# A third stage of seven block products for four recurrent heads, weight sums added up in DRAM, and outputs that may wait for their gates

## The chip, the cores and the metric

The kernel runs on one core of a Trainium2 chip. The metric is the device time of one execution in microseconds (us). A core has five engines with queues of their own: TensorE (PE, matmuls; PEld is its loading of the stationary operand), VectorE (DVE), ScalarE (ACT), GpSimd (POOL) and SyncE (SP). Here SP issues loads and POOL issues stores; both go to the same 16 DMA engines. Matmuls write to PSUM, which this kernel uses as eight tiles of 128x512 words (banks); everything else lies in SBUF or in DRAM.

## The reference

One layer over 1024 tokens of width 1024 in float32. A normalised and modulated input `h` goes through one wide projection. Two recurrences run on its pieces, HGRN2 (8 heads of 128) and GLA (4 heads, keys of 128, values of 256). Each result is normalised, gated and projected, and the two are merged.

```python
h = rms_norm(x, norm_w[l]) * (1.0 + scale[:, None, :]) + shift[:, None, :]
proj = h @ w_in[l]
hq, hf, hi, hz, gq, gk, gv, gz, ga, mg = jnp.split(proj, IN_OFFSETS, axis=-1)
y_h = hgrn2_branch(hq, hf, hi, hz, lb_all[l], hgrn_norm_w[l])
y_g = gla_branch(gq, gk, gv, gz, ga, gla_alpha_w[l], gla_alpha_b[l], gla_norm_w[l])
u_h = y_h @ w_branch[l, 0]
u_g = y_g @ w_branch[l, 1]
mg = jax.nn.sigmoid(mg.reshape(B, T, N_BRANCH, D_MODEL))
merged = mg[:, :, 0] * u_h + mg[:, :, 1] * u_g
x = x + gate[:, None, :] * (merged @ w_out[l])
return rms_norm(x, final_norm_w)
```

In HGRN2 the query is `silu(hq)`, the forget gate `f = lb + (1 - lb) * sigmoid(hf)`, the key `(1 - lb) * sigmoid(-hf)`, and the normalised output is multiplied by `silu(hz)`. GLA's output is multiplied by `silu(gz)`.

## The kernel before

Every large product is taken three times on operands split into a high and a low part (`hi`, `lo`): hi x hi, hi x lo, lo x hi. Making a split costs a cast on ScalarE (`pinned_split`, line 211) and a subtraction on VectorE (line 212). `h` stays split in SBUF, in 16 tiles of `N_SLOTS` = 46 of 4 KB per partition (`Slots`: the slot that was freed longest ago is given out first). A slot may be written again only when its last reader is done, a store included.

There are two ways to multiply. A *feature* (`Feat`, 128 columns of `w_in` for all tokens) takes 8 x 6 = 48 matmuls of 128x512 (line 607) and hands its two PSUM banks to `done`: a query or gate through `silu_done` (sigmoid on ScalarE, product on VectorE), a forget gate through `hf_done`. A *stage of seven block products* computes a 1024x1024 product by 2x2 blocks with seven multiplications instead of eight. For products 5, 3, 6, 7 it needs sums of weight blocks, for 5, 6, 7, 4 differences of blocks of `h`. A stage is 14 jobs (`Vjob`: product `p`, half `kk` of the depth) of 24 matmuls (line 1899). V0 (GLA's values) makes the differences on the way and stores them (`fx`); V1 (HGRN2's values) loads and splits them again. V1's weight sums are made by `v_sums` on VectorE and stored (`vs`).

The jobs run in the order of the list `J`. Beside it `stream.weave` steps two queues of generators, counted in units of six 128x512 matmuls. `stream.side` holds the attention of the 12 heads: scores of a head at four widths (lines 665, 698, 756 and 762, 767), transposes of the keys (791), states (813) and outputs (832, 834). An attention starts when its features are done; at its end `post` multiplies its output by the gate tile, and `put_act` stores it on POOL (`yg`, `yh`). `stream.back` holds work for later: `alpha_side`, `v_sums`, `prepare` and `gate_side`. `prepare` makes the weight sums of the four last stages: 16 times it loads two 512 KB blocks, adds on VectorE (lines 1195 to 1201) and issues four stores on POOL (`ws`, line 1203).

The last stages (`last_stages`, `GROUPS`, matmuls of line 1351) are four more stages of seven products: the two merge gates, then the two branch projections. Stage `b` = 0 fetches blocks of `h` and their differences (`fetch_factor`) and splits them (`build`). Its first two products still run beside the last head, whose score banks `sc_ps` the third, product 5, takes over (`scores_done`). `out_stage` does the output projection.

The scheduler orders the instructions of an engine by their place in the program and by what they need; `held` keeps one where the program has it. Each engine runs its list in order, so an instruction that waits holds all behind it. V0 runs from about 110 to 190 us, GLA's gates and keys to 310, V1 to 420, the last GLA gates and HGRN2 to 806, the last stages to 1110, the output to the end.

## Time and profile before

| what | before |
|---|---|
| median of three runs | 1177.17 us (1176.99 to 1177.36) |
| profiled execution | 1178.0 us |
| its span, first to last instruction | 1176.2 us |
| matmuls recorded | 8137 |
| DMA | 221.44 MB, mean 188 GB/s |
| HBM read, written | 154.57 MB, 65.54 MB |

The page gives for each engine its busy time, in 40 slices the tenths of busy time, and groups of instructions by line and tile: busy time, mean duration, and after the bar the idle time just ahead of them with what ended it. In a timeline a row has its start, its length and how many instructions it merges. A DMA's row gives the time on the issuing engine; its landing is a column of its own.

### The profile page before, as it was taken

The page shows a single profiled execution, that of the slowest core. Times are in us where ns is not written, and L with a number is a line of the kernel's source. Part 1 is how long each engine was busy: PE and PEld are TensorE (multiplying, and loading weights), DVE is VectorE, ACT ScalarE, POOL GpSimd, SP SyncE. Part 2 cuts the span into 40 slices and gives each one's busy share as a digit, 9 for nine tenths or more (in the row PEclk, how much of TensorE's full clock was granted, in tenths as well). Part 3 has the DMA queues.
Part 4 walks back from the last instruction along what each step waited for, and adds up shares of the span by engine and source line. Part 5 has one row for each costly group of instructions (what it writes and reads, how often), then busy time and mean ns, then how long its engine had stood idle before and what let it go on. Part 6 is the DMA issues. An engine that isn't in the chain of part 4 may idle for free.

```text
span 1176.2 us, 20432 instructions
## 1 busy us (share of the span) xinstructions
PE 1156.2 (98%) x8137; PEld 953.1 (81%) x8137; DVE 849.6 (72%) x1347; ACT 589.5 (50%) x903; POOL 125.0 (11%) x261
## 2 busy tenths in 40 slices
PE   7999999999999999999999999999999999999997
PEld 5777888888888788888888878888888888888886
DVE  4754778567665946897897798795643866988994
ACT  4675464663465535433433425567543644534654
POOL 4121111000100212111111010001110000000000
PEclk8999999999999999999999999999999999999999
DMA  9846445255675856565555453247699846434523
GB/s 319 279 149 233 161 170 189 77 165 171 207 260 177 279 189 201 171 203 173 174 184 188 134 205 112 91 162 241 196 314 298 274 156 215 130 108 162 187 90 134
DMA packets 150802, 221.44 MB, mean 188 GB/s; under 512 B 9052, under 2 KB 107410, under 8 KB 150707
## 3 DMA queue, kind: packets, MB, share of 16 engines
q1 hardware_dynamic: 132114, 158.37, 43.2%
q0 software_dynamic: 18544, 61.76, 13.6%
q8 instruction: 64, 1.05, 0.4%
q14 instruction: 32, 0.25, 0.1%
q10 hardware_dynamic: 48, 0.01, 0.0%
HBM read 154.57 MB, written 65.54 MB: 187 GB/s over the span
## 4 chain that ended last, share of the span: by engine, by line
PE 64%; issue 25%; DVE 4%; POOL 3%; DMA 2%; ACT 1%; SPq 0%; POOLq 0%; DVEq 0%; ACTq 0%
PE pd L607 16%; PE pd L1899 11%; PE pd L1351 9%; PE sc_ps L1351 5%; PE pm L1351 4%; PE pd L1528 3%; PE pd L396 3%; PE sc_ps L1528 2%; PE pm L832 1%; PE pm L1528 1%; POOL ws L1203 1%; PE sc_ps L396 1%; PE pm L834 1%; PE pm L813 1%; DMA b<-qk 1%
## 5 line engine op out<-in xcount | busy, mean ns | idle before, releaser
L607 PE MATMUL pd<-b,b 128*128 128x512 f32 x1632 | 391.1, 395 | 0.2 <-DVE b L212 0.2
L607 PEld LDWEIGHTS pd<-b,b 128*128 128x128 f32 x1632 | 302.1, 188 | 64.3 <-DVE b L212 0.6
L1351 PE MATMUL pd<-b,b 128*128 128x512 f32 x720 | 169.8, 390 | 0.1
L1899 PE MATMUL pd<-b,b 128*128 128x512 f32 x672 | 157.5, 393 | 2.6 <-ACT b L211 1.2
L1351 PEld LDWEIGHTS pd<-b,b 128*128 128x128 f32 x720 | 134.8, 188 | 28.5 <-ACT pd L1334 0.5
L1899 PEld LDWEIGHTS pd<-b,b 128*128 128x128 f32 x672 | 125.3, 188 | 30.5 <-ACT b L211 1.6
L212 DVE TENSOR_TENSOR b<-b,b 128x1024 fp32r<-128x1024 f32 x78 | 94.3, 1221 | 35.0 <-ACT b L211 34.7
L1294 DVE TENSOR_TENSOR b<-b,b 128x1024 fp32r<-128x1024 f32 x56 | 68.4, 1225 | 68.5 <-ACT b L1293 54.4
L1293 ACT CAST b<-b 128x1024 fp32r<-128x1024 f32 x56 | 58.5, 1049 | 69.5 <-PE pm L1351 17.0
L211 ACT CAST b<-b 128x1024 fp32r<-128x1024 f32 x78 | 79.8, 1047 | 12.1 <-DMA v<-b 3.9
L1351 PE MATMUL sc_ps<-b,b 128*128 128x512 f32 x324 | 77.2, 390 | 0.0
L1270 ACT CAST b<-b 128x1024 fp32r<-128x1024 f32 x48 | 49.7, 1049 | 46.5 <-PE pd L1351 16.0
L1351 PE MATMUL pm<-b,b 128*128 128x512 f32 x300 | 71.1, 389 | 0.0
L1351 PEld LDWEIGHTS sc_ps<-b,b 128*128 128x128 f32 x324 | 60.7, 188 | 12.6
L1271 DVE TENSOR_TENSOR b<-b,b 128x1024 fp32r<-128x1024 f32 x48 | 58.0, 1226 | 17.0 <-ACT b L1270 11.5
L1351 PEld LDWEIGHTS pm<-b,b 128*128 128x128 f32 x300 | 56.3, 188 | 11.7
L718 ACT COPY xb<-b 128x512 f32<-128x512 f32 x48 | 29.7, 621 | 55.8 <-DVE b L700 18.9
L1203 POOL DMA_DIRECT2D ws<-b x64 | 34.8, 545 | 190.6 <-DVE b L1195 118.7
L203 DVE TENSOR_TENSOR b<-b,b 128x1024 fp32r<-128x1024 f32 (+1 forms) x37 | 35.9, 984 | 26.4 <-ACT b L202 26.3
L396 PE MATMUL pd<-b,b 128*128 128x512 f32 x192 | 51.9, 403 | 0.5 <-ACT b L202 0.4
L832 PE MATMUL pm<-scT,b 128*128 128x128 f32 x256 | 46.9, 275 | 0.5 <-DVE b L819 0.5
L396 PEld LDWEIGHTS pd<-b,b 128*128 128x128 f32 x192 | 34.3, 188 | 11.6 <-ACT b L202 1.5
(316 smaller groups left out, 1713.3 us busy)
## 6 DMA issues: line engine op xcount, KB each, us to landing
b<-in_w_in_dram SPq DMA_DIRECT2D x72, 512.0 KB, 4.1
ws<-b POOLq DMA_DIRECT2D x64, 256.0 KB, 3.6
b<-ws SPq DMA_DIRECT2D x32, 512.0 KB, 4.6
b<-in_x_dram SPq DMA_DIRECT2D x16, 512.0 KB, 4.2
b<-in_ada_w_dram SPq DMA_DIRECT2D x32, 256.0 KB, 6.5
v<-b POOLq DMA_DIRECT2D x32, 256.0 KB, 4.3
b<-v SPq DMA_DIRECT2D x16, 512.0 KB, 5.0
b<-fx SPq DMA_DIRECT2D x16, 512.0 KB, 4.6
```

The lines of the kernel that those rows point to most:

```text
L211: held(nc.scalar.copy(hi, src))
L212: nc.vector.tensor_sub(lo, src, hi.bitcast(F32))
L396: nc.tensor.matmul(accs[f], wg(a, d, f), b[d][:, half * 512:half * 512 + 512], start=(d == 0 and n == 0), stop=(d == KT - 1 and n == 2))
L607: nc.tensor.matmul(ps[th][0:w, :], a[:, k, 0:w], b[:, th * 512:(th + 1) * 512], start=(k == 0 and n == 0), stop=(k == KT - 1 and n == 2))
L832: nc.tensor.matmul(o, vch(ch)[:, vh * P:(vh + 1) * P], scT[:, ch, :], start=True, stop=(ch == 0))
L1270: nc.scalar.copy(hi, src)
L1271: nc.vector.tensor_sub(lo, src, hi.bitcast(F32))
L1293: nc.scalar.copy(hi, t)
L1294: nc.vector.tensor_sub(lo, t, hi.bitcast(F32))
L1351: nc.tensor.matmul(o, a[:, sl], c, start=(p in (1, 5) and kt == 0 and n == 0), stop=(kt == 3 and n == 2), skip_group_check=True)
L1528: nc.tensor.matmul(o, a, b, start=(p in (1, 5) and kt == 0 and n == 0), stop=(kt == 3 and n == 2), skip_group_check=True)
L1899: nc.tensor.matmul(st.bank[i], x_, w_, start=(p in (1, 5) and kk == 0 and a == 0 and n == 0), stop=(kk == 1 and a == 1 and n == 2), skip_g ...
```

## The change

1. *A third stage.* Queries and forget gates of HGRN2's heads 0 to 3 are no longer eight features. They are a third stage (`Fstage(2)`) whose weight blocks hold 256 columns of queries and 256 of forget gates. Its 14 jobs run behind V1, with the weights as the stationary operand. Results go to DRAM (`f_d`), queries through silu; `load_qf` loads them for a head and `make_fk` makes forget gate and key from the raw gate.
2. *Split activations in DRAM.* V0 stores its differences already split (`xp_d`); V1, the third stage and the first of the last stages load both parts instead of splitting.
3. *Weight sums in DRAM.* `v_sums` (for V1 and the third stage) and `prepare` no longer load, add and store. POOL issues transfers from DRAM to DRAM, plain and adding, along `CHAIN`, each waiting for the one that it builds on.
4. *Outputs that wait.* If a gate tile isn't there when an attention ends, the scaled output is kept (`late`) and multiplied when the gate comes (`settle`). So GLA's four attentions start one behind the other, and gates of GLA's heads 2, 3 and HGRN2's 0 to 3 come behind the third stage.
5. `silu` is one function on ScalarE instead of sigmoid and product. The key's scaling moves to ScalarE. `gate_side` loads two rows ahead.

```diff
+    def minus_split(src):
+        hi, lo = (S.get(list(src.shape[1:]), F32R) for _ in range(2))
+        held(nc.scalar.activation(hi, src, AF.Copy, scale=-1.0))
+        nc.vector.scalar_tensor_tensor(lo, src, -1.0, hi.bitcast(F32), ALU.mult, ALU.subtract)
+        return hi, lo
...
-                nc.scalar.activation(s[:, sl], ps[th], AF.Sigmoid)
-                nc.vector.tensor_mul(s[:, sl], s[:, sl], ps[th])
+                nc.scalar.activation(s[:, sl], ps[th], AF.Silu)
...
+    def settle(store, key):
+        if key in scaled and key in store:
+            acts_, d, y = late.pop(key)
+            z = store.pop(key)
+            nc.vector.tensor_mul(y, y, z)
+            S.free(z)
+            put_act(acts_, d, y)
...
+    def load_qf(h):
+        for z, name in enumerate(("q", "raw")):
+            t = h_state[name, h] = S.get([T])
+            nc.sync.dma_start(t, f_d[h][z])
+
+    def make_fk(h):
+        f, k = h_state.pop(("raw", h)), S.get([T])
+        nc.scalar.activation(k, f, AF.Sigmoid, scale=-1.0)
+        nc.scalar.activation(f, f, AF.Sigmoid)
+        nc.vector.tensor_scalar(f, f, oml[:, h:h + 1], lb[:, h:h + 1], ALU.mult, ALU.add)
+        nc.vector.tensor_scalar_max(f, f, F_FLOOR)
+        nc.scalar.activation(k, k, AF.Copy, scale=oml[:, h:h + 1])
+        h_state["f", h], h_state["k", h] = f, k
...
+    CHAIN = ((7, (0, 0)), (5, (0, 1)), (7, (0, 1)), (5, (1, 1)), (6, 7), (6, (1, 1)), (3, 6), (3, (1, 0)))
...
+        for b in range(4):
...
+            for p, src in CHAIN:
+                while paused[0]:
+                    yield 1
+                first = p not in done
+                done.add(p)
+                if isinstance(src, int):
+                    held(nc.gpsimd.dma_start(w_sums[b][p], w_sums[b][src]))
+                else:
+                    for i, x in enumerate(block(*src)):
+                        x = x.rearrange("(k p) f -> p k f", p=P)
+                        y = w_sums[b][p][:, i].rearrange("p (k f) -> p k f", f=P)
+                        if first:
+                            held(nc.gpsimd.dma_start(y, x))
+                        else:
+                            held(nc.gpsimd.dma_start(y, x, accum_op=ALU.add))
+                        yield 0.5
+                yield 1.5
...
+    def load_parts(p, kk):
+        x = [S.get([2, 512], F32R) for _ in range(2)]
+        for z in range(2):
+            nc.sync.dma_start(x[z].bitcast(F32).rearrange("p a t -> p (a t)"), xp_d[p][kk][z])
+        return x
...
     def fetch_factor(g):
...
+            H[g] = list(zip(*[load_parts(p, kk) for kk in range(2)]))
...
                 if p not in RAW_X:
-                    self.x = pinned_split(self.x_raw)
-                    S.free(self.x_raw)
+                    self.x = load_parts(p, kk)
...
+                    if st.s > 1:
+                        moved = ((w_hi, x_hi), (w_hi, x_lo), (w_lo, x_hi))
...
     def first_head():
-        start_side(gla_attention(0))
+        for h in range(4):
+            start_side(gla_attention(h))
...
-    vjobs[1][12].begins = lambda: pause(False)
+    vjobs[2][12].begins = lambda: pause(False)
...
     J.extend(vjobs[0])
-    for h in range(3):
-        if h == 2:
-            J.append(gla_k[2])
-        J.extend(gla_z[h, vh] for vh in range(2))
-    J.append(gla_k[3])
+    J.extend(gla_z[h, vh] for h in range(2) for vh in range(2))
+    J.extend(gla_k[h] for h in (2, 3))
     J.extend(vjobs[1])
-    J.extend(gla_z[3, vh] for vh in range(2))
-    J.extend(hgrn)
+    J.extend(vjobs[2])
+    J.append(hgrn[2])
+    J.extend(gla_z[h, vh] for h in (2, 3) for vh in range(2))
+    J.extend(hgrn[3 * h + 2] for h in (1, 2, 3))
+    J.extend(hgrn[12:])
```

Three places show how instructions move. The names are tiles, `b` a slot's tile; the numbers tell tiles apart and are not the same in the two kernels. First POOL in the middle of `prepare`. Before, stores of sums out of SBUF, with the stores of one head's output between them:

```order
L1203 DMA ws_804<-b_5087 128x512
L904 DMA yh_129<-b_4793 128x512
L904 DMA yh_133<-b_4793 128x512
L1203 DMA ws_801<-b_5086 128x512
L1203 DMA ws_802<-b_5086 128x512
L1203 DMA ws_803<-b_5087 128x512
```

Now the end of the first block's chain, from its adding transfers of products 7 and 5 on (`ws_796`, `ws_793`; 6 is `ws_794`, 3 is `ws_795`), and the start of the next:

```order
L1273 DMA ws_796<-in_w_in_dram 128x4x128 x4
L1273 DMA ws_793<-in_w_in_dram 128x4x128 x4
L1265 DMA ws_794<-ws_796 16x16384
L1273 DMA ws_794<-in_w_in_dram 128x4x128 x4
L1265 DMA ws_795<-ws_794 16x16384
L1273 DMA ws_795<-in_w_in_dram 128x4x128 x4
L912 DMA yh_129<-b_4585 128x512
L912 DMA yh_133<-b_4585 128x512
L1271 DMA ws_800<-in_w_in_dram 128x4x128 x4
L912 DMA yg_123<-b_3382 128x512
L912 DMA yg_127<-b_3382 128x512
```

Each group needs the one above that wrote its tile or its source, and the stores of outputs stand in the same queue. Second SP in V1, where the products 6, 7 and 4 are loaded. Before, one tile of weights (`vs`, `in_w_in`) and one of differences (`fx`) for a job:

```order
L1838 DMA b_3234<-vs_847 128x1024
L1838 DMA b_3180<-vs_844 128x1024
L1843 DMA b_3236<-fx_781 128x1024
L1838 DMA b_3290<-vs_848 128x1024
L1843 DMA b_3292<-fx_782 128x1024
L1843 DMA b_3352<-fx_783 128x1024
L1840 DMA b_3350<-in_w_in_dram 128x2x512
```

Now two tiles of split differences (`xp`) beside one of weights, and values for an attention between:

```order
L1294 DMA b_3041<-xp_783 128x1024
L1294 DMA b_3042<-xp_784 128x1024
L1930 DMA b_3122<-in_w_in_dram 128x2x512
L1294 DMA b_3135<-xp_786 128x1024
L1012 DMA b_3144<-v_831 128x4x256
L1294 DMA b_3134<-xp_785 128x1024
L1012 DMA b_3146<-v_831 128x4x256
L1930 DMA b_3226<-in_w_in_dram 128x2x512
L1294 DMA b_3241<-xp_788 128x1024
```

Third TensorE in the first of the last stages, around the last scores of the last head (767 before, 773 now), which go to `sc_ps_73`. Before, the rows behind those scores; 36 matmuls of line 1351 stand there until `sc_ps` is taken over:

```order
L767 MATMUL sc_ps_73<-b_7171,b_7340 64x64 x8
L1351 MATMUL pd_0_7505<-b_7527,b_7600 128x512
L1351 MATMUL pd_0_7505<-b_7529,b_7600 128x512
L1351 MATMUL pd_0_7505<-b_7527,b_7601 128x512
L1351 MATMUL pd_0_7505<-b_7527,b_7600 128x512
L1351 MATMUL pd_0_7505<-b_7529,b_7600 128x512
```

Now (773 for 767, 1419 for 1351, 797 for 791):

```order
L773 MATMUL sc_ps_73<-b_7105,b_7241 64x64 x8
L1419 MATMUL pd_0_7381<-b_7410,b_7565 128x512
L1419 MATMUL pd_0_7381<-b_7412,b_7565 128x512
L1419 MATMUL pd_0_7381<-b_7410,b_7566 128x512
L1419 MATMUL pd_0_7381<-b_7410,b_7565 128x512
L1419 MATMUL pd_0_7381<-b_7412,b_7565 128x512
L1419 MATMUL pd_0_7381<-b_7410,b_7566 128x512
L797 MATMUL pm_7730<-ident,b_7241 128x128 x4
L797 MATMUL pm_7736<-ident,b_7241 128x128 x3
L1419 MATMUL sc_ps_72<-b_7586,b_7611 128x512
L1419 MATMUL sc_ps_72<-b_7587,b_7611 128x512
L1419 MATMUL sc_ps_73<-b_7586,b_7611 128x512
```

The head stands 30 matmuls later, and product 5's first matmuls into `sc_ps` follow its scores closely.

301 lines of the change are left out of this document (170 added, 131 removed).

## The prediction

> **What bounds the kernel now.** I read the page from the top: busy shares, then the granted clock.
>
> ```profile
> span 1176.2 us, 20432 instructions
> PE 1156.2 (98%) x8137; PEld 953.1 (81%) x8137; DVE 849.6 (72%) x1347; ACT 589.5 (50%) x903; POOL 125.0 (11%) x261
> PEclk8999999999999999999999999999999999999999
> ```
>
> TensorE is busy in 98% of the span at a granted clock of nine tenths or more. A busy TensorE need not be dense, so next comes the view by stretches. Its columns are length, then busy time and instruction count of PE, PEld, DVE, ACT and POOL, then clock, DMA share and GB/s. The first five stretches are stage V0, the features after it, stage V1, the heads of the second branch, and the first of the last stages; the sixth is a plain stretch of 128x512 matmuls.
>
> ```profile
> 110.00:190.00 80.00, 79.20 (x459) 64.62 (x462) 63.99 (x78) 39.65 (x53) 15.65 (x29) 1.00 0.55 191
> 190.00:310.00 120.00, 119.52 (x943) 100.42 (x931) 79.92 (x135) 60.93 (x90) 5.88 (x11) 1.00 0.44 137
> 310.00:425.00 115.00, 112.80 (x975) 93.04 (x974) 80.63 (x145) 67.03 (x102) 16.69 (x31) 1.00 0.72 243
> 425.00:806.00 381.00, 379.92 (x3659) 316.89 (x3658) 305.17 (x580) 168.66 (x296) 44.00 (x81) 1.00 0.53 167
> 806.00:890.00 84.00, 83.93 (x386) 69.69 (x385) 44.21 (x44) 44.03 (x60) 12.34 (x23) 1.00 0.80 268
> 880.00:1080.00 200.00, 200.00 (x884) 165.64 (x883) 146.81 (x154) 95.01 (x118) 3.73 (x7) 1.00 0.59 196
> ```
>
> Two things are to be seen. The last row gives the price of one matmul in a dense stream: 200 us / 884 = 0.226 us. And between 110 and 806 us TensorE idles only 0.80 + 0.48 + 2.20 + 1.08 = 4.6 us. So the time is the number of matmuls times 0.226 us, plus small change. Whatever leaves TensorE shortens the kernel; whatever leaves another engine does not, unless it ends one of those 4.6 us; and whatever makes TensorE wait lengthens it at once.
>
> **The change part by part.** *Matmuls.* Eight features of 48 matmuls (384) give way to a stage of 7 products x 2 halves x 24 (336). Counted over the whole order, 48 matmuls of 128x512 go and nothing else on TensorE changes in number. 48 x 0.226 = **-10.9 us**. Swapping the stationary and the moved operand in the new stage leaves both at 128x128 and 128x512, so that price stays.
>
> *Idle time that may go.* The largest idle of TensorE in the middle lies in V1:
>
> ```profile
> 384.47 4.82 ACT L211 CAST b<-b 128x1024 fp32r<-128x1024 f32 x5
> 386.50 0.82 PE L1899 MATMUL pd<-b,b 128*128 128x512 f32 x2 [1.17 <-ACT b L211]
> 387.95 2.35 PE L1899 MATMUL pd<-b,b 128*128 128x512 f32 x9 [0.64 <-DVE b L212]
> ```
>
> Five casts stand in a row on ScalarE, and TensorE waits 1.17 + 0.64 us for them and for the subtraction behind. They split weights and activations. The activations now come split from DRAM, so 8 of the stage's 22 splits go. Bounds are 0 and -4.6 us (all the idle time above); I take **-1.0**, half of these two waits, because casts of weights stay behind the same queue.
>
> *More bytes in V1 and the third stage.* A job of a built product (5, 6, 7, 4) loads 512 KB of weights and now twice 512 KB of split activations: 1.57 MB in 24 x 0.226 = 5.4 us, 290 GB/s, where it was 193. The stores add four times 256 KB per product (10.9 us), 97 GB/s: 387 in all. What the DMA can give is shown by the fullest rows of 20 us (columns as above), and by the 40 slices of the stretch 310 to 425 us, whose best is 412:
>
> ```profile
> 840.00:860.00 20.00, 20.00 (x90) 16.58 (x89) 17.28 (x18) 10.70 (x15) 6.65 (x13) 1.00 0.80 265
> 860.00:880.00 20.00, 19.93 (x89) 16.16 (x88) 4.51 (x4) 7.05 (x10) 2.25 (x5) 1.00 0.86 290
> 880.00:900.00 20.00, 20.00 (x90) 16.57 (x89) 12.01 (x11) 10.15 (x15) 1.61 (x3) 1.00 0.99 332
> GB/s 279 342 198 285 412 229 219 291 324 353 191 326 219 232 133 57 306 1 6 0 68 342 323 358 296 94 159 261 270 408 393 392 367 291 193 300 333 106 324 36
> ```
>
> At 332 GB/s a built product's 4.2 MB takes 12.6 us against 10.9, 1.8 us late; eight such products over both stages make the upper end, 14 us. The lower end is 0: a whole stage moves 14 x 0.52 + 8 x 1.05 + 16 x 0.26 = 19.9 MB in 76 us, 262 GB/s; weights are fetched up to four jobs ahead and activations two, and TensorE stayed full at 332. I take **+1.0**, near the lower end. SP issues these loads in order, so behind a late one the next job's weights wait too; that is inside the 14.
>
> *More bytes in the first of the last stages.* Four products now fetch 2.1 MB of split activations instead of 1.05: 4.2 MB more between 840 and 900. The three rows above leave (0.20 + 0.14 + 0.01) x 20 us x 332 GB/s = 2.3 MB of room; the other 1.9 MB are 5.7 us at 332, the upper end. The lower is 0, since the stores of gates and output weights in that stretch are awaited by nobody there and can slide. I take **+1.0**. The casts and subtractions of these four builds go, but neither engine is waited for in these rows.
>
> *The last head stands later.* Its last score matmuls now end six matmuls and seven transposes ahead of product 5, which reuses their PSUM banks; before, 36 matmuls lay between. What must be over first:
>
> ```profile
> 794.28 0.69 PE L767 MATMUL sc_ps<-b,b 128*64 128x64 f32 x16
> 795.40 0.69 DVE L726 TENSOR_TENSOR b<-b,tot 128x512 f32<-128x512 f32 x1
> 796.01 0.69 DVE L727 TENSOR_TENSOR b<-b,tot 128x512 f32<-128x512 f32 x1
> 796.61 0.30 DVE L771 COPY_PREDICATED blk<-mask,sc_ps 128x128 f32<-128x128 int32 x1
> 797.00 0.74 ACT L779 COPY scT<-sc_ps 64x256 f32<-64x256 f32 x2 [1.52 <-DVE blk L771]
> 797.78 0.93 PE L791 MATMUL pm<-ident,b 128*128 128x128 f32 x7
> ```
>
> From the scores' end (794.97) to the copies' end (797.74) it is 2.8 us; cover is 6 x 0.226 + about 0.8 for the transposes + two matmuls into the other bank, 2.6 us. Bounds are 0 and 1.4 (transposes held up too); I take **+0.3**, the difference with a little for the queues.
>
> *ScalarE* gets 14 more table loads:
>
> ```profile
> 105.66 1.28 ACT L924 ACT_TABLE_LOAD   x1
> ```
>
> That is 18 us more on an engine busy 50%. They stand ahead of reads of PSUM by the features, whose banks come in two pairs, so a read has a feature (48 x 0.226 = 10.9 us) of slack: nothing, and 1.3 us for each load if that cover went. *Late gate tiles.* The product of a waiting output with its gate is issued only behind the gate's feature, so on VectorE nothing queues behind an open wait; on POOL its two stores have the chain of sums behind them, whose slack follows. The next head's forget gate is made from the loaded tile while 36 matmuls still lie ahead of that head's scores: nothing for both.
>
> *Sums in DRAM.* No row shows a transfer from DRAM to DRAM, or one that adds. The nearest rows:
>
> ```profile
> L1203 POOL DMA_DIRECT2D ws<-b x64 | 34.8, 545 | 190.6 <-DVE b L1195 118.7 <-DVE b L1201 29.5 <-DVE b L1197 14.7
> L357 POOL DMA_DIRECT2D blk<-in_w_in_dram x2 | 1.9, 936 | 0.0
> b<-in_w_in_dram SPq DMA_DIRECT2D x72, 512.0 KB, 4.1
> ws<-b POOLq DMA_DIRECT2D x64, 256.0 KB, 3.6
> 425.00:806.00 381.00, 284.06 (x1189) 219.46 (x1187) 1.00 0.53 167
> ```
>
> An issue costs POOL 0.55 us (128 rows) to 0.94 us (1024 short rows). The last row is the stretch of the heads for the features' matmuls alone: six of them, one step of the program's clock, take 6 x 381 / 1189 = 1.92 us with attention in between. The program spreads one block's chain over 24 steps, 46 us. The chain has six rounds that wait for each other. Lower end: 6 x 3.6 = 22 us and some issues, less than 46, no lag. Upper end: 8.4 MB read, 8.4 written and 4.2 read again by the additions, 21 MB at 332 GB/s = 63 us, plus six landings of 4.1, 87 us; 41 us of lag per block, 164 after four. What is behind it on POOL: the stores of gated outputs, whose buffers are taken again 21 to 32 steps later, 40 to 61 us, by the next weights and tiles. So the bounds are 0 and 164 - 50 = 114 us. I take **0**: 512 KB in short rows land in 4.1 us at half load, far nearer the lower end. The sums themselves are needed only from 820 us, so nothing waits for them.
>
> The Trainium skill ("DMA: Bandwidth & Descriptors", section on the anatomy of one DMA on the GpSimd path) fits such a transfer as 2.0 us plus bytes / 436 GB/s, an estimate here of 2.6 us for 256 KB; the row above has 3.6 us. By it six rounds are some 20 us, and the sum stays as it is. A rule of the Trainium skill against the change ("SBUF — State Buffer", section on who interferes with whom): VectorE in its two-port modes locks GpSimd out while it writes descriptors. The row's 545 ns with VectorE busy 72% shows no such stretch, and by the rule these issues would lag by single VectorE instructions.
>
> *Sum.* The profiled execution took 1178.0 us, 1.8 over its span. -10.9 - 1.0 + 1.0 + 1.0 + 0.3 = -9.6 gives 1168.4 us; the median of the runs lies 0.8 lower, so the forecast is **1167.5 us**.
>
> **The rivals.**
> - *The chain of sums falls behind.* For it: six dependent rounds, an in-order POOL queue, outputs' buffers held by it. Against: the landings above, and DMA half idle there (0.53). It decides from 46 + 50 / 4 = 59 us per block; at 65 us the lag is 4 x 19 - 50 = 26 us, **1194 us**, slower than before.
> - *Bytes decide.* About half of the upper ends (7 of 14, 3 of 5.7) instead of 1 each: **1176 us**. For it: 387 GB/s asked. Against: prefetch.
> - *More idle time goes*, as fewer splits and no sums on VectorE end all 4.6 us, and nothing new waits: 1177.2 - 10.9 - 4.6 = **1162 us**. Against: the order on TensorE still puts scores 36 matmuls behind a head.
> - *The 48 matmuls do not go*: excluded, they are gone from the order.
>
> **How the numbers follow.** The forecast (1163 to 1172) gets 0.62, bytes (1172 to 1179.5) 0.16, the chain 0.12, idle time (1161 to 1163) 0.08, and 0.02 is for slower by something not seen here. The range 1161 to 1179 leaves out the chain and little else. A measurement of this kernel tells 0.2%, 2.4 us, from no change: faster is below 1174.8, the forecast, the idle case and 0.07 of bytes, 0.77; same gets 0.08; slower 0.15.
>
> **What would show it.** Right: 48 fewer matmuls at 0.226 us; an idle of TensorE in the middle near 5 us; stores of outputs on POOL that wait for VectorE or ScalarE rather than for a sum. Wrong: TensorE waiting in V1, in the third stage or around 830 to 890 us for loads of split activations (bytes); SP loads or casts waiting for output stores in the features after the third stage, with the sums' landings above 8 us (chain); a wait before the first matmul of product 5 above 1.4 us (last head).

## Result, and the profile after

The changed kernel takes **1234.4 us** (median of four runs, 1233.2 to 1236.7) beside 1177.3 us (1177.0 to 1179.5) for the kernel before on the same chip: ratio 1.0483, interval 1.0463 to 1.0503. It is 57 us slower, where 10 us less were forecast. The page of the profiled execution, its lines that answer to those of before, and of its DMA queues the one that GpSimd feeds:

```profile
span 1232.3 us, 20289 instructions
...
PE 1155.0 (94%) x8089; PEld 949.5 (77%) x8089; DVE 762.5 (62%) x1212; ACT 620.0 (50%) x937; POOL 249.1 (20%) x361
...
PEclk9999998999999999799799997999999999999999
...
q0 software_dynamic: 59312, 99.51, 32.1%
```

The 48 matmuls are gone (8137 to 8089), and VectorE has 87 us less to do. But TensorE idles in 6% of the span, where it was 2%, POOL's work has doubled, and its queue carries 99.5 MB. The clock dips in four slices. The view by stretches (columns as in the prediction) shows where:

```profile
184.00:197.00 13.00, 3.13 (x62) 2.61 (x64) 6.37 (x10) 2.17 (x3) 0.00 (x0) 0.71 0.87 316
197.00:230.00 33.00, 33.00 (x323) 26.97 (x315) 22.08 (x50) 15.01 (x28) 10.18 (x14) 0.96 0.87 220
480.00:530.00 50.00, 38.71 (x405) 32.00 (x404) 31.84 (x64) 22.89 (x38) 21.55 (x22) 0.86 1.06 236
530.00:584.00 54.00, 54.00 (x544) 44.91 (x543) 26.99 (x55) 21.19 (x35) 30.93 (x33) 1.00 1.06 223
584.00:640.00 56.00, 42.22 (x427) 35.19 (x426) 32.75 (x69) 27.10 (x43) 25.32 (x27) 0.88 1.05 218
640.00:731.00 91.00, 88.81 (x881) 72.85 (x880) 47.87 (x97) 36.20 (x63) 38.05 (x38) 1.00 0.97 204
731.00:800.00 69.00, 48.52 (x510) 39.67 (x509) 47.03 (x91) 32.16 (x52) 5.22 (x8) 0.85 0.43 107
880.00:1080.00 200.00, 199.12 (x879) 164.53 (x878) 125.14 (x127) 92.24 (x120) 13.91 (x26) 1.00 0.72 242
```

Four stretches lose 9.9, 11.3, 13.8 and 20.5 us of TensorE; between them it is nearly full, and in the last stages it runs as before (199.12 / 879 = 0.227 us). Behind a stop the granted clock stays low for a while: 0.96 over the second row, and cut finer 0.53 from 195.5 to 200 us and 1.00 from 200 us on. That costs a few us more. The waits of TensorE name what came last at each stop (waited for; total, times, longest):

```profile
PE sc_ps L704 <- DVE xb L700: 33.8, 3, 19.7
PE sc_ps L671 <- issue: 9.9, 1, 9.9
PE sc_ps L762 <- ACT xb L724: 7.5, 1, 7.5
```

These are score matmuls of attention heads (L671, L704, L762) that start late. For the longest, the waits between 728 and 752 us lead back step by step, to be read from the last row up:

```profile
ACT b L1183 <- DMA yh<-b: 28.3, 1, 28.3
DVE b L1188 <- ACT b L1183: 24.4, 1, 24.4
...
PE sc_ps L704 <- DVE xb L700: 19.7, 1, 19.7
```

VectorE stands behind L1188, which needs ScalarE's L1183, the square of the head's output; that instruction writes into a slot that a store of an earlier output (yh) still reads. The timeline of POOL there (start, length, then idle before it and its releaser) shows why the store is late:

```profile
710.44 5.08 POOL L1273 DMA_DIRECT2D ws<-in_w_branch_dram  x4 [16.97 <-DMA ws<-ws]
722.09 0.54 POOL L1265 DMA_DIRECT2D ws<-ws  x1 [6.57 <-DMA ws<-in_w_branch_dram]
727.84 5.07 POOL L1273 DMA_DIRECT2D ws<-in_w_branch_dram  x4 [5.22 <-DMA ws<-ws]
730.84 3.21 POOL L912 DMA_DIRECT2D yh<-b  x2
```

POOL issues in order. Three times it stands and waits until a step of the chain of sums has landed; the two stores of yh come behind all of it, at 730.84, though the last product of L1188 ahead of them had ended at 674.5. ScalarE has wanted the slot since 711.7, and goes on when the stores have landed, at 739.99. The stop at 585 us shows the sign that the prediction gave for its rival, the chain that falls behind: a load on SyncE that waits for a store of an output, with landings of the sums above 8 us. The rows are SyncE's load of the next head's forget gate and ScalarE's sigmoid behind it:

```profile
SPq L1149 <- DMA yg<-b: 13.9, 1, 13.9
ACT L1153 <- DMA b<-f: 16.5, 1, 16.5
```

That store of yg was not late on POOL alone. POOL issued it at 567.0 us, behind eight adding DMAs and a copy of the chain; it landed 13.5 us after its issue, and those adding DMAs 7.6 to 19.5 us after theirs. So the chain delays a store twice, in its turn on POOL and in its landing. The whole chain, in POOL's waits:

```profile
POOL ws L1273 <- DMA ws<-ws: 67.5, 8, 17.0
...
POOL ws L1265 <- DMA ws<-in_w_in_dram: 28.1, 4, 8.9
...
POOL ws L1265 <- DMA ws<-in_w_branch_dram: 26.9, 4, 9.3
```

The first DMAs of the four blocks start at 474, 536, 604 and 663 us and the last is issued by 733: 62, 68, 59 and 70 us per block, 65 in the mean.

For sums over the whole kernel I priced each matmul at the median interval between two starts for its width in the kernel before, and counted what lies above. The prices add up to 1123.9 us before and 1113.0 after: 10.9 less. Intervals more than 0.4 us over the price hold 11.9 us before, **71.9 us** after. Below, "stops" is this last number; the length of a single stop is the whole interval between two starts.

### The profile page after: what moved, and what is told of

Its sections match the earlier page's. It is cut to its first block, busy times and chain, and to the rows that moved or that the text cites. A ratio compares the mean times of both kernels' runs of the same rounds, so it can differ in the third digit from the quotient of the medians.

```text
span 1232.3 us, 20289 instructions
## 1 busy us (share of the span) xinstructions
PE 1155.0 (94%) x8089; PEld 949.5 (77%) x8089; DVE 762.5 (62%) x1212; ACT 620.0 (50%) x937; POOL 249.1 (20%) x361
## 3 DMA queue, kind: packets, MB, share of 16 engines
q0 software_dynamic: 59312, 99.51, 32.1%
## 4 chain that ended last, share of the span: by engine, by line
PE 35%; issue 33%; DMA 21%; POOL 8%; DVE 2%; ACT 1%; SPq 1%; POOLq 0%; ACTq 0%; DVEq 0%
PE pd L1419 9%; DMA ws<-ws 6%; PE pd L613 5%; DMA ws<-in_w_branch_dram 5%; PE sc_ps L1419 5%; DMA ws<-in_w_in_dram 5%; PE pm L1419 4%; PE pd L1596 3%; POOL ws L1273 3%; PE pd L1990 2%; PE sc_ps L1596 2%; PE pm L1596 1%; DMA xp<-b 1%; POOL v L1856 1%; DMA yh<-b 1%
## 5 line engine op out<-in xcount | busy, mean ns | idle before, releaser
L613 PEld LDWEIGHTS pd<-b,b 128*128 128x128 f32 x1248 | 233.5, 191 | 49.5
L1990 PEld LDWEIGHTS pd<-b,b 128*128 128x128 f32 x1008 | 188.4, 189 | 43.7 <-issue 1.4
L1419 PEld LDWEIGHTS pd<-b,b 128*128 128x128 f32 x720 | 134.8, 188 | 29.4 <-ACT pd L1402 1.3
L1362 DVE TENSOR_TENSOR b<-b,b 128x1024 fp32r<-128x1024 f32 x56 | 68.2, 1221 | 65.0 <-ACT b L1361 51.9
L212 DVE TENSOR_TENSOR b<-b,b 128x1024 fp32r<-128x1024 f32 x72 | 87.3, 1220 | 31.9 <-ACT b L211 27.4
L1361 ACT CAST b<-b 128x1024 fp32r<-128x1024 f32 x56 | 58.4, 1049 | 73.9 <-PE pm L1419 17.0
L211 ACT CAST b<-b 128x1024 fp32r<-128x1024 f32 x72 | 74.3, 1045 | 7.2 <-issue 3.2
L1338 ACT CAST b<-b 128x1024 fp32r<-128x1024 f32 x40 | 41.4, 1050 | 37.6 <-PE pd L1419 15.1
L1339 DVE TENSOR_TENSOR b<-b,b 128x1024 fp32r<-128x1024 f32 x40 | 48.1, 1219 | 14.2 <-ACT b L1338 10.3
L732 DVE TENSOR_TENSOR b<-b,tot 128x512 f32<-128x512 f32 x36 | 24.7, 686 | 40.2 <-PE sc_ps L773 29.4
L1273 POOL DMA_DIRECT2D ws<-in_w_branch_dram x32 | 41.5, 2235 | 36.9 <-DMA ws<-ws 36.2
L1273 POOL DMA_DIRECT2D ws<-in_w_in_dram x32 | 41.5, 2204 | 31.3 <-DMA ws<-ws 31.3
```

The source lines that it names most:

```text
L211: held(nc.scalar.copy(hi, src))
L212: nc.vector.tensor_sub(lo, src, hi.bitcast(F32))
L613: nc.tensor.matmul(ps[th][0:w, :], a[:, k, 0:w], b[:, th * 512:(th + 1) * 512], start=(k == 0 and n == 0), stop=(k == KT - 1 and n == 2))
L1273: held(nc.gpsimd.dma_start(y, x, accum_op=ALU.add))
L1339: nc.vector.tensor_sub(lo, src, hi.bitcast(F32))
L1361: nc.scalar.copy(hi, t)
```

## The experiments

Seventeen runs, in the order in which they ran. The ratio is to the kernel before, measured beside it; that kernel took 1177.3 to 1179.7 us from chip to chip, so a difference in us between runs of two chips is good to some 2 us.

| run | edit | us | ratio, interval | stops |
|---|---|---|---|---|
| (change) | | 1234.4 | 1.0483 (1.0463 to 1.0503) | 71.9 |
| e1_prep_vector | last sums on VectorE, later | 1195.0 | 1.0131 (1.0103 to 1.0158) | 36.7 |
| e2_vsums_vector | stage sums on VectorE | 1238.1 | 1.0507 (1.0491 to 1.0523) | 74.2 |
| e3_both_vector | both | 1197.0 | 1.0160 (1.0137 to 1.0183) | 37.5 |
| e4_paced | chain spread out | 1212.7 | 1.0281 (1.0254 to 1.0308) | 45.7 |
| e5_factors_raw | no pairs | 1221.8 | 1.0359 (1.0337 to 1.0382) | 59.4 |
| e6_qk_early | first head's load earlier | 1230.5 | 1.0435 (1.0408 to 1.0461) | 67.3 |
| e7_no_add | chain copies, adds nothing | 1203.7 | 1.0200 (1.0172 to 1.0228) | 43.6 |
| e8_both_earlier | e3 earlier, and e6 | 1185.5 | 1.0052 (1.0033 to 1.0071) | 28.8 |
| e9_both_raw | e3 earlier, and e5 | 1190.8 | 1.0096 (1.0080 to 1.0113) | 26.8 |
| e10_even_raw | chain even and earlier, and e5 | 1200.3 | 1.0175 (1.0160 to 1.0190) | 39.1 |
| e11_before_chain | kernel before, with the chain | 1227.3 | 1.0414 (1.0393 to 1.0435) | 59.1 |
| e12_fk_own_head | forget gate by its own head | 1220.6 | 1.0363 (1.0329 to 1.0398) | 67.4 |
| e13_same_pace | last sums on VectorE, chain's pace | 1194.1 | 1.0123 (1.0102 to 1.0143) | 34.5 |
| e14_same_pace_raw | e13 and e5 | 1180.1 | 1.0025 (1.0011 to 1.0038) | 22.6 |
| e15_same_pace_qk | e13 and e6 | 1189.3 | 1.0094 (1.0079 to 1.0109) | 25.6 |
| e16_raw_fk_own | e13, e5 and e12 | **1172.0** | **0.9943** (0.9924 to 0.9963) | 12.1 |
| e17_raw_fk_held | e13, e5, gate's sigmoids pinned | 1181.9 | 1.0021 (1.0008 to 1.0035) | 22.0 |

**Is it the chain?** Four runs put the sums back on VectorE, in the one place or in the other, or spread the chain.

```diff
 # e1: prepare() of the kernel before; e2: v_sums() likewise; e3: both
-    held(nc.gpsimd.dma_start(y, x, accum_op=ALU.add))
+    held(add(parts[5], x1[:, :, 1], x2[:, :, 1]))
...
+    nc.gpsimd.dma_start(w_sums[b][p][:, i], parts[p].rearrange("p k f -> p (k f)"))
 # e1, e3, e4: order of the side tasks
-    stream.back.append([prepare(), 4, 1, 0])
     stream.back.append([gate_side(), 4, 1, 0])
+    stream.back.append([prepare(), 4, 1, 0])
 # e4: pause behind each step of the chain
-                yield 1.5
+                yield 6
```

> The changed kernel, with the sums for the last four block products made by VectorE in SBUF again, as before the change (loads on SyncE, four additions, four stores on GpSimd's queue); the gate row's small task goes ahead of them, so that both end in time. The sums of the second and third stage stay as DMAs that add in DRAM. Theory A (the chain of adding DMAs fills GpSimd's queue and the stores of the heads' outputs stand behind it, so that slots, loads and then TensorE wait): the gaps of 7.9, 14.2 and 20.1 us (and 2.2 ahead of them) go with the 7 us or so that the lower clock behind them costs, the gap of 10.3 us at 184.9 us stays: 1234 - 51 = 1183 us (1176 to 1192). Rival B (the heads' new order: the next head's sigmoids and the late gate tiles stall ScalarE whoever makes the sums): 1222 us or more. Rival C (the bytes of the change, whichever queue moves them): 1215 us or more.

> The changed kernel, with the sums of the second and third stage (values of the late heads, and queries and forget gates) made by VectorE in SBUF, as the one before did for the second stage; the chain of adding DMAs for the last four block products stays. Theory A: only the gap of 10.3 us at 184.9 us goes, with 2 us of clock: 1222 us (1217 to 1229), the three later gaps stay. Rival B: 1222 as well, or no change at all where that gap is the first head's own. Rival C: bytes in the first 200 us fall, 1222 or so.

> Both of the last two edits: no DMA adds in DRAM any more, all else of the change stays (third stage of block products, factors kept as pairs, late gate tiles, ScalarE's silu and sigmoids). Theory A: no gap above 3 us is left, 1171 us (1165 to 1178), below the kernel before (1177). Rival B: 1210 us or more, with the gaps where ScalarE waits for a load of a head's forget gate. Rival C: the traffic of the pairs and of the third stage is still there, 1190 us or more.

> The changed kernel with the same adding DMAs, but 6 units of the program (in place of 1.5) between two steps of the chain for the last four block products, so about 15 us between steps where a step's DMAs need 8 to 18 us from the first issue to the last landing; the gate row's task goes ahead of the chain. Nothing is left out. Theory A in its first form (GpSimd's queue stands waiting for a step to land, and stores behind it wait too): most of the three gaps go, 1190 us (1180 to 1205). Theory A in its second form (the issue of an adding DMA, 2.2 us on GpSimd, and the room that it takes in the DMA queue are what costs, and spreading only moves it): 1210 to 1234 us. Rival B: 1222 us or more.

With the last four products' sums on VectorE (e1) the three late stops are gone and 39 us are won; new ones of 5.5, 1.7 and 2.9 us stand at 808 to 893 us, so it ended above its range, but far below what rivals B and C had (1222 and 1215 us or more). The stage sums (e2) cost nothing as adding DMAs: on VectorE the kernel is no faster. The stop at 185 us stayed in all four: it isn't the sums, against what theory A had for e2 and e3. So e3 came to e1's time, 26 us above what it was to show, with stops of 9.2 us at 186 and 6.3 and 3.3 us at 809 and 869 us. That is a time that rival C, the change's other bytes, had given for it; the pairs among them and the late sums are taken up below. Spread out (e4), the same DMAs leave no stop over 1 us between 484 and 809 us, where the heads run, but they now run to 968 us, and stops of 2.3, 4.4, 7.8 and 2.7 us stand between 865 and 980 us in the last stages. 1212.7 us is in the range of theory A's second form, that spreading only moves the cost.

The reverse is the clearest: the chain alone, put into the kernel before.

```diff
 # e11: the kernel before
-    def prepare():
+    def prepare():            # the chain, body as in the changed kernel
...
+                while stream.units < 210:
+                    yield 1
```

> The kernel before, with only its sums for the last four products replaced by the changed kernel's chain of adding DMAs, from unit 210 of the program on, where the heads with forget gates begin, as in the changed kernel. Nothing is left out. Theory A (the chain alone is the cause): gaps of 8 to 20 us at two or three heads, 1177 + 35 to 50 = 1212 to 1227 us. Rival B' (it takes the chain together with the change's longer life of the heads' outputs and with forget gates loaded from DRAM): 1190 us or less.

It costs 48 us, at the upper end of theory A, and nearly all of it in one stop of 45 us at 616 us, where two or three of 8 to 20 us were expected. The waits there, of the engines and then of SyncE's queue:

```profile
DVE b L1072 <- DMA b<-in_ada_w_dram: 45.3, 1, 45.3
PE pd L607 <- ACT b L211: 45.0, 1, 45.0
```

```profile
SPq L1068 <- DMA yh<-b: 45.1, 1, 45.1
```

TensorE waits for ScalarE, VectorE stands at L1072 of the gate row's task for a load, and that load stands in SyncE's queue behind the landing of a store of yh, whose slot it takes. Here the stores' rows on POOL, between two blocks of the chain:

```profile
627.37 5.07 POOL L1204 DMA_DIRECT2D ws<-in_w_branch_dram  x4 [5.17 <-DMA ws<-ws]
630.36 4.33 POOL L1202 DMA_DIRECT2D ws<-in_w_branch_dram  x3
632.60 3.19 POOL L904 DMA_DIRECT2D yh<-b  x2
```

They land at 642.9 us, and SyncE's load goes out then. So it takes neither late gate tiles nor forget gates from DRAM: rival B' falls. What differs from kernel to kernel is the victim (a square on ScalarE, a load of forget gates or of the gate row on SyncE).

**What in the chain is dear?** One run leaves the additions out and keeps everything else of the chain.

```diff
-                            held(nc.gpsimd.dma_start(y, x, accum_op=ALU.add))
+                            held(nc.gpsimd.dma_start(y, x))
```

> The changed kernel with the adding DMAs of the last four block products replaced by plain copies of the same shape, in the same order and with the same waits on the step before: the additions of those sums are left out. Theory A, adding is the price (the issue of an adding DMA takes 2.2 us on GpSimd where a plain one of the same shape takes 1.2 to 1.9, and its landing 8 to 9 us): chain per block from 65 us to 45 us or less, gaps mostly gone, 1195 us (1185 to 1210). Theory A, the order is the price (copies from DRAM to DRAM that wait for each other in GpSimd's queue, with the heads' stores behind them): block time stays above 55 us, 1222 us or more.

Its time lies in the range of the first case, 30.7 us below the change; its block time, below, lies between the two cases. The groups of POOL, of the change and then of e7, and e7's row of the DMA queue (busy us, mean ns of one; durations of neighbours overlap, so busy time over count is the better price):

```profile
L1273 POOL DMA_DIRECT2D ws<-in_w_in_dram x32 | 41.5, 2204 | 31.3 <-DMA ws<-ws 31.3
...
L912 POOL DMA_DIRECT2D yh<-b x16 | 16.2, 1293 | 108.8 <-DVE b L1188 108.8
```

```profile
L1273 POOL DMA_DIRECT2D ws<-in_w_in_dram x32 | 24.7, 778 | 23.9 <-DMA ws<-ws 21.4 <-DMA ws<-in_w_in_dram 1.7 <-DMA f<-b 0.6
...
L912 POOL DMA_DIRECT2D yh<-b x16 | 8.9, 554 | 138.2 <-DVE b L1188 136.5 <-DVE b L732 1.6
```

```profile
q0 software_dynamic: 30640, 99.51, 25.8%
```

An adding DMA of 256 KB keeps POOL for 41.5 / 32 = 1.30 us, a plain one for 24.7 / 32 = 0.77; my "9 us for four" in the expectations was the mean duration times four, while four in a row take 5.1. With the same bytes the queue has 30640 packets instead of 59312. A block takes 51 us in the mean (starts at 476, 532, 588 and 632 us, end at 679) instead of 65, and of the late stops only the first stays, 8.5 us at 499 us, with others of 3.0 us at 587 and 2.7 us at 826. Both halves of theory A hold in part: the additions turn 51 us into 65, and in this kernel the damage lies mostly between those two.

The first stop comes where the chain begins, beside the place where the second head's forget gates are loaded from DRAM just behind their own stores. It needs the chain but not the additions: e13 below, without the chain, has no stop over 1 us between 484 and 549 us, and in e4, where the chain begins 61 us later, it isn't there either. In the change ScalarE waits there 10.0 us for a load of forget gates that lands 15.2 us after its issue (the eight such loads have a median of 5.3), while the DMA engines are full: their share is 1.05 from 480 to 498 us. That points to what is on the way, rather than to a store's turn on POOL; no run parts the two for this stop.

**The stop at 185 us.** In the change's trace SyncE waits there for a slot that a store of values still reads, before it can issue the second load of the first head's queries and keys at 174.3 us. That load lands 15.7 us later, and ScalarE waits for it; the third row is ScalarE's in e5, without pairs:

```profile
SPq L1060 <- DMA v<-b: 9.9, 1, 9.9
```

```profile
ACT xb L663 <- DMA b<-qk: 12.3, 1, 12.3
```

```profile
ACT xb L663 <- DMA b<-qk: 1.6, 1, 1.6
```

```diff
 # e5: factors once, as they are; stages and last product split them again
-                for z in range(2):
-                    nc.gpsimd.dma_start(xp_d[p][kk][z], self.x[z].bitcast(F32).rearrange("p a t -> p (a t)"))
+        nc.gpsimd.dma_start(fx_d[p][kk], xq[dst][kk].rearrange("p a t -> p (a t)"))
 # e6
-    vjobs[0][10].begins = lambda: load_qk(0)
+    vjobs[0][8].begins = lambda: load_qk(0)
```

> The changed kernel without the part that keeps factors as pairs: the first block stage stores the eight factors once as they are (8 stores of 512 KB, as before the change, in place of 16 of the split halves), and the second and third stage and the last one load and split them again. The chain of adding DMAs stays. At issue is the gap of 10.3 us at 184.9 us, which stood in every run so far (9.2 to 10.9 us, with and without adding DMAs for the second stage). Theory D1 (the pairs' stores fill GpSimd's queue, stores of values behind them keep slots, and SyncE waits for such a slot with the first head's queries): that gap goes with 2 us of clock, and the splits cost nothing on TensorE: 1222 us (1216 to 1230). Rival D2 (slots are short at that place for other reasons of the change, its deeper loading ahead or the forget gates' side task moved from unit 72 to 20): the gap stays, 1234 us or more.

> The changed kernel with one edit: the first head's queries and keys are loaded two half products earlier (at the start of the ninth of fourteen, not of the eleventh; 23 us earlier). Under D1 and D2 alike the gap of 10.3 us at 184.9 us goes if the load's issue is all that is late: 1222 us (1218 to 1230). If the bytes on the way are what is late there (the loads landed 16 us after their issue where 4 us is usual), the load would get through in time as well but another takes its place, and 3 us or less is won: 1231 us or more. The three later gaps stay.

Without the pairs the stop is gone and the kernel 12.6 us faster, as D1 had it. The earlier load alone wins 3.9 us, between its two cases: part of the stop moves with it (1.6 us at 162 and 3.3 us at 184 us are left). So the pairs are the cause. With their sixteen 512 KB stores in the first stage the four stores of values issued between 177 and 181 us land in 7.7 to 8.8 us; in e5, with eight stores, those issued between 178 and 182 us land in 5.4 to 6.1. That the stores do it, rather than the slots that hold the pairs until they are stored, is argued from this: no run parts the two.

**What is left without the chain?** The sums on VectorE could go earlier or be spaced otherwise, so a few runs looked for what remains.

```diff
 # e8, e9: sums may begin in the third stage
-    vjobs[2][12].begins = lambda: pause(False)
+    vjobs[1][12].begins = lambda: pause(False)
 # e8, e9: yield 7 -> 4 behind a block; e13 to e17: yield 3, start and order as in the changed kernel
 # e10: chain kept
-                        yield 0.5
-                yield 1.5
+                        yield 1.5
+                yield 0.5
```

> All sums on VectorE as in the run with both, which came to 1197 us with a gap of 9.2 us at 185.7 us and gaps of 6.3 and 3.3 us at 809 and 869 us; now the sums for the last four products may begin 56 units earlier (in the third stage) and are spaced by 4 units, not 7, so that they end ahead of the last heads, and the first head's queries and keys are loaded two half products earlier. Theory A with both leftovers as mere lateness: 1197 - 12 - 13 = 1172 us (1166 to 1180), which would be the forecast's own sum without the adding DMAs. Rival C (bytes and slots, wherever they are put): the gaps come back elsewhere, 1185 us or more.

> No DMA adds, and no pairs: all sums on VectorE (those of the last four products from the third stage on, spaced by 4 units), the eight factors stored once and split again by each stage; the first head's queries load where the changed kernel loads them. Of the change there are left the third stage, the late gate tiles and ScalarE's share of the head's work. The run with pairs and the same sums came to 1185.5 us beside 1179.5 for the kernel before, with 5 us of waits in 130 to 230 us. If pairs cost only there, 1181 us (1176 to 1186); if the further splits (1.2 us of VectorE each) on an engine that also makes the sums delay the heads, 1188 us or more.

> The changed kernel with the adding DMAs for the last four products kept, but issued evenly (1.5 units of the program after each one, 2.9 us, in place of four within 2 units and a pause) and from the third stage on (56 units earlier), and with the factors stored once and split again. Theory A, now more exactly (an adding DMA takes 2.3 us of GpSimd to issue where a plain copy takes 0.74, four in a row shut the queue for 9 us, and whatever the heads store waits): with one adding DMA each 2.9 us the queue is still 80% taken in those steps, so part of the gaps remains: 1200 us (1185 to 1215). If only the waits on the step before matter, no gap over 3 us is left: 1180 us. If the place matters (third stage beside heads), gaps appear in 370 to 480 us, where there were none.

e8 has no stop over 3.4 us behind the first 20 us and is still at 1185.5: by its time the second of its cases, though no large gap has come back elsewhere. e9, at 1190.8 us, came out as its second case, with a stop of 4.3 us in the third stage, where its sums now stand beside the further splits; TensorE waits there for ScalarE's casts. e10, at the value given for theory A, wins 21.5 us over e5, but stops of 7.5, 8.3 and 5.1 us stay: even with one DMA per 1.5 units POOL waits 64 us for `ws<-ws`, and some stops move into the third stage, as its last case had it. What tells parts from places is e13: one edit, the same units as the chain.

> The changed kernel with one edit: the sums for the last four block products are made by VectorE, in the same place and at the same pace as the chain (the four blocks end at units 234, 258, 282 and 306 of the program, the chain's at 233, 257, 281 and 305), with the gate row behind them as in the changed kernel. The first run with VectorE's sums (1195 us) had them 54 to 105 units later, and gaps of 5.5, 1.7 and 2.9 us beside the last head. If those were that lateness, they go, and the gap of 10 us at 185 us stays: 1195 - 12 = 1183 us (1178 to 1189). If VectorE is too full for the sums at this pace (65 us for a block, with two heads' work), gaps of several us appear in 480 to 760 us: 1190 us or more.

> The last one, with the factors stored once and split again by each stage (no pairs). The pairs' part cost 12.6 us in the changed kernel (1234.4 to 1221.8): 1183 - 12 = 1171 us (1166 to 1180), below the kernel before at 1177 to 1180. If VectorE lacks room once it makes the sums and the further splits (as in the run with all sums on VectorE and no pairs, 1190.8 us), 1183 us or more.

> The one with VectorE's sums at the chain's pace and with pairs, and with the first head's queries and keys loaded two half products earlier. That edit alone took the changed kernel from 1234.4 to 1230.5 us and the gap of 10.3 us to two of 1.6 and 3.3 us: 1183 - 5 = 1178 us (1173 to 1184), level with the kernel before.

e13 stands at 1194.1: **the chain is worth 40 us** in this kernel. It is no better than e1: the stops beside the last head are 1.2 and 1.6 us now, but one of 5.8 us stands at 550 us, as its second case had it. Without pairs (e14) another 14.0 us go, to the end of the range given; the earlier load (e15) wins 4.8 us, about the 5 expected, but from 1194 us instead of 1183, so it ended above its range. In e14 one stop of 4.9 us is left in the heads. ScalarE's timeline there, and TensorE's waits for the copies L798 in the whole run (total, times, longest):

```profile
536.95 1.28 ACT L1153 ACT_TABLE_LOAD   x1 [4.08 <-DMA b<-in_w_branch_dram]
538.25 1.06 ACT L1153 ACTIVATE b<-b 128x1024 f32<-128x1024 f32 x1
539.33 0.75 ACT L785 COPY scT<-sc_ps 64x256 f32<-64x256 f32 x2
540.09 1.28 ACT L975 ACT_TABLE_LOAD   x1
541.39 1.08 ACT L975 ACTIVATE b<-pd 128x512 f32<-128x512 f32 x2
542.36 0.97 ACT L798 COPY b<-pm 128x512 f32<-128x512 f32 x2
```

```profile
PE pm L821 <- ACT b L798: 7.5, 6, 4.5
```

L1153 is the next head's sigmoid. It waits 4.1 us with the running head's copies (L785, L798) behind it, and it changes ScalarE's table twice. Three runs took it away, the first still with the chain:

```diff
 # e12, e16: at the end of hgrn_attention(h); each head then makes its own, with yield 2
-        if h + 1 in stored:
-            make_fk(h + 1)
 # e17: in make_fk
-        nc.scalar.activation(k, f, AF.Sigmoid, scale=-1.0)
-        nc.scalar.activation(f, f, AF.Sigmoid)
+        held(nc.scalar.activation(k, f, AF.Sigmoid, scale=-1.0))
+        held(nc.scalar.activation(f, f, AF.Sigmoid))
```

> The changed kernel with one edit: each head makes its own forget gate and keys when it begins, in place of the head ahead of it making them for the next one before its own last step; ScalarE then has no sigmoid that waits for the next head's load in front of the running head's copies. Rival B (that order on ScalarE is what turns a late load into a gap): the gaps of 7.9 and 14.2 us go, 1234 - 25 = 1209 us, while the one of 20.1 us (a square that waits for a slot which a store still reads) stays. Theory A (the store and the slot behind the chain are late whatever ScalarE's order): gaps move but their sum stays within 10 us, 1224 to 1244 us.

> VectorE's sums at the chain's pace, no pairs (that came to 1180.1 us), and each head makes its own forget gate and keys when it begins. Left in the run without this edit was a gap of 4.9 us at 538 us, where ScalarE's sigmoid for the next head waited 4.1 us for a load in front of the running head's copies, with a table load of 1.28 us on each side. Rival B in small: that gap goes, 1175 us (1170 to 1179), under the kernel before. If the load is late whoever waits for it, the gap moves to the head's own start: 1180 us or more.

> The same without that edit, but with the two sigmoids pinned to their place in the program, so that the scheduler no longer puts them ahead of the running head's copies (the second head's stands 4 rows later in ScalarE's order, the third's 13 to 14). Rival B in small: the gap of 4.9 us goes and nothing comes in its place, 1174 us (1169 to 1178). If it is the load's lateness: 1180 us or more.

With the chain (e12) it is undecided: the median falls by 13.8 us, to below theory A's range, but in the profiled execution, a slower one of 1226.8 us span, the three late stops still hold 40.5 us (42.1 in the change). Without the chain it decides: e16 wins 8.2 us over e14 (9.7 by the ratios), and behind a stop of 2.9 us at 470 us, where the third stage ends, its heads run without one over 1.5 us. Pinning alone (e17) wins nothing; smaller stops (2.5, 1.5, 1.4, 1.4 us) stand between 515 and 608 us instead, partly at the next head's start. So order alone isn't it; a head that makes its gate itself also gets two units between the sigmoid and its first scores, and the runs don't part these two.

e16 beats both kernels, by 0.57% (interval 0.37 to 0.76) the one before. Its page and stretches of the heads and of the last stages:

```profile
span 1166.9 us, 20480 instructions
...
PE 1146.2 (98%) x8089; PEld 944.1 (81%) x8089; DVE 826.6 (71%) x1300; ACT 641.5 (55%) x959; POOL 167.5 (14%) x313
```

```profile
470.00:795.00 325.00, 322.00 (x3357) 267.41 (x3356) 266.47 (x514) 177.10 (x288) 50.61 (x94) 0.99 0.67 218
...
880.00:1080.00 200.00, 200.00 (x884) 165.62 (x883) 150.46 (x161) 93.75 (x113) 3.05 (x6) 1.00 0.56 185
```

TensorE is busy 98% again, with 48 matmuls less. It keeps the third stage, the late gate tiles and the stage sums as adding DMAs; it gives up the chain, the pairs and the sigmoids ahead of time.

## Why the prediction was wrong

**Sums in DRAM: taken as 0, measured 40 us (e13) to 48 us (e11).** This is the step that failed: "I take 0: 512 KB in short rows land in 4.1 us at half load, far nearer the lower end". That row was of loads into SBUF on SyncE's queue. In the chain 256 KB pieces (one in three a plain copy, the others adding) land in a median of 8.3 and 9.4 us, the copies between sums in 7.3, and a block takes 65 us instead of at most 46. The Trainium skill ("DMA: Bandwidth & Descriptors", section on the anatomy of one DMA on the GpSimd path) gives by its fit an estimate of 2.6 us for 256 KB; no landing median of the chain comes near it, so the measurement decides. (At 2.6 us six rounds would be 15.6 us; the prediction's "some 20" goes by the row's 3.6.) The rival was described rightly, down to its sign (stores behind the chain on POOL, landings above 8 us) and even to the 65 us of its example; its point of decision, 59 us per block, lies between e7 (51 us) and the change (65 us). But e11 stops for 45 us at 57 us per block (starts at 463, 514, 571 and 630 us, end at 690), so 59 is no threshold for another kernel.

Its price was also too low: 26 us of lag for 65 us per block, where 40 were lost. The slack of 40 to 61 us was that of one slot, and about right: at the longest stop the slot was wanted 37 us after its product (711.7 against 674.5). But a late store stops an engine that works in order, and everything behind it: SyncE's further loads in e11, ScalarE and through it VectorE in the change. So the lag is paid at several heads, and the clock behind each stop comes on top. The prediction also counted only the stores' turn on POOL, not that loads and stores beside the chain land late (15.2 us for a load, 13.5 for a store, at the first two of the late stops).

**Next head's forget gate: taken as "nothing", measured 8.2 us** (e14 to e16, without the chain). The prediction counted the matmuls ahead of that head's scores, not who stands behind the sigmoid on ScalarE while it waits for its load.

**More bytes in V1 and the third stage: +1.0 with an upper end of 14; the pairs cost 12.6 to 14.0 us** (e5, e14). In the two stages named (288 to 487 us in the change) the one stop above 1.3 us, 2.2 us at 482, waits for VectorE (L667) and not for a load, so the step's reasoning held there; the cost came in the stage ahead, where the pairs are written, on POOL's queue, which the step hadn't counted.

**Right:** 48 matmuls are worth 10.9 us, by the prices of the intervals, and e16 shows most of it as time: the span of its profiled execution is 9.3 us under that of before (the medians differ by 6.8), with stops of 12.1 us beside 11.9. The idle time in V1 (-1.0) did go. The rows are of before and of the change:

```profile
300.00:400.00 100.00, 98.19 (x751) 81.44 (x750) 70.48 (x112) 57.80 (x82) 13.43 (x25) 1.00 0.71 237
```

```profile
300.00:400.00 100.00, 100.00 (x727) 84.60 (x726) 60.58 (x104) 54.57 (x83) 15.07 (x25) 1.00 0.84 270
```

That the split activations from DRAM did it isn't shown: e16, which splits again, idles no more there (105.00 of 105 us busy from 310 to 415). The first of the last stages (+1.0) has one stop over 1 us in the change, 1.3 us at 933 us; the last head (+0.3) shows 1.2 and 0.9 us at 857 to 859 us, about its upper bound of 1.4.

From the change to e16 it is 1234.4 - 40.3 (chain, e13) - 14.0 (pairs, e14) - 8.2 (sigmoids, e16) = 1172 us, 4 us above the forecast. Each term is the step from one run to the next, so that they add up says nothing by itself, and e16 is no test of the forecast's sum: without pairs, its -1.0 and both its +1.0 have no object. The range left out the chain's case, at a chance of 0.12, though its bounds, 0 and 114 us, came from no row of its kind.

## What to carry to other kernels

A chain of DMAs that wait for each other doesn't run "in the background" when it shares an in-order queue with stores: price it by its own landings and by those of what shares the DMA engines with it, and ask for each store behind it which slot it holds and which engine, in order, waits for that slot. Adding DMAs were free for the sums of the two stages (e2) and cost 40 us beside the heads; that nothing urgent stood behind the former is likely, and no run shows it. Where the trace has no row of an operation's kind, measure it or keep its whole range.

## Of the hardware, not expected

An adding DMA is dearer than its bytes: per 256 KB 1.30 us of POOL against 0.77 for a copy, about twice the packets for the queue as a whole (59312 against 30640), and landings of 8.3 and 9.4 us against 6.6 and 7.0 for all of the chain's 256 KB pieces, of which two in three add. Ordinary stores in the same queue suffer with it: the stores of yh land in a median of 7.6 us in the change, 4.4 in e7 and 3.7 in the kernel before. And a stop of TensorE lowers the granted clock beyond its own end: matmuls run again from 195.2 us, at a clock of 0.53 until 200 us, where dense stretches have 1.00; behind the longest stop it is 0.50 from 752 to 756 us.
